# A two-layer hybrid block on one core: the sums over gate and up weights on VectorE, and weights split 1024 columns at a time

## The chip, the core and the metric

The kernel runs on one core of one Trainium2 chip. The core's engines have their own instruction queues, and each queue runs in order: PE (TensorE) multiplies matrices, DVE (VectorE), ACT (ScalarE) and POOL (GpSimd) work element by element, SP issues the DMAs. The metric is the device time of one execution in microseconds (us); lower is better.

## What is computed

Two layers over 512 tokens of 1024 features, in fp32. Each layer has two gated feed-forward networks, a token mixer of three kinds of heads between them, and a small gated embedding at its end. Only the feed-forward networks matter here; there are four, two a layer.

```python
D_MODEL, SEQ, DEPTH, D_FF = 1024, 512, 2, 2816

def swiglu(x, w_in, w_out):
    gate, up = jnp.split(x @ w_in, 2, axis=-1)
    return (jax.nn.silu(gate) * up) @ w_out

for l in range(DEPTH):
    x = x + 0.5 * rms_norm(swiglu(rms_norm(x, ln_ffn1_pre[l]), w_ffn1_in[l], w_ffn1_out[l]), ln_ffn1_post[l])
    mix = token_mixing(rms_norm(x, ln_mix_pre[l]), ...)
    x = x + rms_norm(mix, ln_mix_post[l])
    x = x + 0.5 * rms_norm(swiglu(rms_norm(x, ln_ffn2_pre[l]), w_ffn2_in[l], w_ffn2_out[l]), ln_ffn2_post[l])
    gate = jax.nn.sigmoid(rms_norm(x, ln_ple_pre[l]) @ w_ple_gate[l])
    x = x + rms_norm(gate * (p[l] @ w_ple_proj[l]), ln_ple_post[l])
```

## The kernel before

**Products in three parts.** Every fp32 operand of a large product is split into a high part (fp32r) and a low part, the rest: `split` (L140, L141) has ACT write the high part and DVE, or another engine if it is given, subtract it from the source. A product is then three matmuls (`mm3`, L162 to L164): high x high, high x low, low x high. A split of weights goes into a buffer of the pool `wsp`, tag `w`, which has NW buffers: six, for 512 columns each.

**The first product of a network** has 22 units (tiles), each of 128 gate and 128 up features. It goes by Winograd's form of Strassen's algorithm: instead of eight products of 128x512x256 there are seven, numbered 1 to 7, of 12 matmuls each (four blocks of inputs by three parts), so 84 in a unit. The price is sums. Those over inputs (`tx`) are made once for a network, in `turn`. Those over weights are made in each unit: from the raw weights g1, g2, u1, u2 (two tiles of a slot, 128x1024 each, by DMA) POOL makes s1 = u1 + u2 (L353), s2 = s1 - g1 (L354), s3 = g1 - u1 (L355) and s4 = g2 - s2 (L356), 512 columns each, into tiles `ws`. Products 1 and 2 take g1 and g2 as they are, 6, 7, 5, 3 and 4 take s2, s3, s1, s4 and u2. Each of the seven is split on its own, 512 columns.

**What comes out** is combined by DVE from PSUM: L362, L365, L367, L369, L370, L373, then ACT's silu (L371), then gate times up (L376). A PSUM bank serves two products: the first matmul of product 3 must wait until DVE has read product 6 out of the same bank (L362). ACT copies product 1 out (L347).

**What sets the order.** The program is written unit by unit; a scheduler then places the instructions on each queue, so DVE's queue mixes splits of the next unit with additions of this one. Nothing overtakes on a queue. Three of six raw slots (tag `q`) hold weights during the units; the other three hold `tx`. The first four units (G = 4) are loaded early, in `ffn_begin`, while the phase before ends, and their products 1 are given the splits that are made there, three or four of them by POOL; `NP1` and `flush` say between which of them the last tiles of tokens are turned and summed (`turn`).

**The second product** (`ffn_out`) goes pair by pair of feature tiles and by halves of the columns. Fourteen pairs of a network go by the seven products, with sums over features by POOL (`left`, L426 to L429), sums over weights by POOL and DVE (`right`, L448 to L450), and splits of the raw weights in two pieces of 256 and 512 columns (`wb`). The others are plain (`wblock`), split in two pieces of 512.

## Time and profile before

| | us |
|---|---|
| runs, median of 3 (lowest, highest) | 2371.92 (2371.49, 2373.13) |
| span of the profiled execution | 2369.3 |
| four networks, units 4 to 20 of each, a unit | about 11.2 |
| PE busy, DVE busy, POOL busy | 2142.1, 2019.5, 1215.5 |

The three runs were timed without the profile; the profiled execution is told by its span, from the first to the last instruction, which is 2.6 us below their median. The page's groups add up instructions of one line and shape: first the count, then busy time in us and the mean of one in ns, then the engine's idle time before them and what ended it.

```profile
L141 DVE TENSOR_TENSOR w<-wr,w 128x512 fp32r<-128x512 f32 x249 | 374.8, 1528 | 10.0 <-ACT w L140 9.8
L141 DVE TENSOR_TENSOR w<-ws,w 128x512 fp32r<-128x512 f32 x352 | 327.7, 935 | 3.2 <-ACT w L140 3.1
L354 POOL TENSOR_TENSOR ws<-ws,wr 128x512 f32<-128x512 f32 x88 | 147.4, 1675 | 0.6
```

Here `w` is a split's buffer, `wr` the raw weights, `ws` a sum, and `fp32r<-` the written and read types. Busy times overlap a little at their ends, so an operation's cost in a full queue is read from one start to the next.

### The profile page before, as it was taken

What the parts mean: (1) busy time and instruction counts of PE and PEld (TensorE: products, weight loads), DVE (VectorE), ACT (ScalarE), POOL (GpSimd) and SP (SyncE); (2) the same over time, 40 slices, a digit from 0 to 9 for tenths busy, and PEclk for the clock granted to TensorE, in tenths of its full rate; (3) what the DMA queues carried; (4) which work ended last, traced back from release to release, by engine and by line L of the source; (5) the groups of instructions that cost most, each with busy time, mean ns of one, the idle gap of its engine ahead of it and who ended that gap; (6) DMA issues with size and microseconds to landing.
All of it is one profiled execution on the core that took longest, in us unless ns stands there. A gap on an engine that the chain in (4) does not pass through costs nothing. (4 is left out here: it accounts for less than half of the span.)

```text
span 2369.3 us, 42540 instructions
## 1 busy us (share of the span) xinstructions
PE 2142.1 (90%) x16592; PEld 1975.2 (83%) x16592; DVE 2019.5 (85%) x2990; ACT 1159.0 (49%) x2262; POOL 1215.5 (51%) x1088
## 2 busy tenths in 40 slices
PE   5899988999998899988989989889999989989898
PEld 5888887988778888887878888888887789889787
DVE  8999999645768999998689999986557699999984
ACT  4444544546545444545554445444474454445443
POOL 5665476132236665566365655751332466555751
PEclk8999999999999999999999999999999999999999
DMA  3222222422031222123411221233220312222232
GB/s 151 90 89 90 71 90 90 147 81 55 20 142 54 86 93 90 63 90 116 134 71 72 92 105 55 84 120 122 68 63 7 143 72 90 90 90 75 78 107 80
DMA packets 67513, 208.78 MB, mean 88 GB/s; under 512 B 15728, under 2 KB 16752, under 8 KB 67312
## 3 DMA queue, kind: packets, MB, share of 16 engines
q1 hardware_dynamic: 67312, 206.07, 25.2%
q8 instruction: 130, 2.13, 0.4%
q14 instruction: 71, 0.58, 0.1%
HBM read 199.23 MB, written 6.82 MB: 87 GB/s over the span
## 5 line engine op out<-in xcount | busy, mean ns | idle before, releaser
L162 PE MATMUL p<-xh,w 128*128 128x256 f32 x1408 | 407.8, 291 | 79.8 <-DVE gate L362 77.5
L164 PE MATMUL p<-xh,w 128*128 128x256 f32 x1408 | 401.6, 286 | 13.6 <-DVE w L141 13.6
L163 PE MATMUL p<-xl,w 128*128 128x256 f32 x1408 | 400.8, 285 | 0.1
L141 DVE TENSOR_TENSOR w<-wr,w 128x512 fp32r<-128x512 f32 x249 | 374.8, 1528 | 10.0 <-ACT w L140 9.8
L140 ACT ACTIVATE w<-ws 128x512 fp32r<-128x512 f32 x352 | 210.6, 623 | 305.0 <-POOL ws L354 178.2
L162 PEld LDWEIGHTS p<-xh,w 128*128 128x128 f32 x1408 | 269.9, 192 | 95.5 <-DVE gate L362 89.7
L141 DVE TENSOR_TENSOR w<-ws,w 128x512 fp32r<-128x512 f32 x352 | 327.7, 935 | 3.2 <-ACT w L140 3.1
L162 PE MATMUL p<-tx,w 128*128 128x256 f32 x1056 | 299.9, 285 | 19.1 <-ACT tx L140 14.7
L164 PE MATMUL p<-tx,w 128*128 128x256 f32 x1056 | 298.9, 284 | 5.3 <-DVE w L141 5.2
L163 PE MATMUL p<-tx,w 128*128 128x256 f32 x1056 | 299.2, 284 | 4.7 <-DVE tx L141 4.7
L164 PEld LDWEIGHTS p<-xh,w 128*128 128x128 f32 x1408 | 270.9, 192 | 14.8 <-DVE w L141 14.8
L353 POOL TENSOR_TENSOR ws<-wr 128x512 f32<-128x512 f32 x88 | 119.0, 1352 | 316.2 <-issue 299.5
L163 PEld LDWEIGHTS p<-xl,w 128*128 128x128 f32 x1408 | 270.8, 192 | 0.7 <-DVE xl L141 0.7
L162 PEld LDWEIGHTS p<-tx,w 128*128 128x128 f32 x1056 | 204.7, 194 | 21.2 <-ACT tx L140 15.3
L164 PEld LDWEIGHTS p<-tx,w 128*128 128x128 f32 x1056 | 203.3, 193 | 7.4 <-DVE w L141 7.1
L163 PEld LDWEIGHTS p<-tx,w 128*128 128x128 f32 x1056 | 203.7, 193 | 5.6 <-DVE tx L141 5.6
L466 PE MATMUL y<-wo,hq 128*128 128x256 f32 x1536 | 189.4, 282 | 3.2 <-DVE up L373 2.7
L140 ACT ACTIVATE w<-wr 128x512 fp32r<-128x512 f32 x264 | 163.3, 625 | 57.7 <-PE p L164 41.9
L466 PEld LDWEIGHTS y<-wo,hq 128*128 128x128 f32 x1536 | 184.5, 189 | 4.8 <-DVE up L373 3.5
L355 POOL TENSOR_TENSOR ws<-wr 128x512 f32<-128x512 f32 x88 | 145.9, 1658 | 46.7 <-DVE w L141 45.0
L354 POOL TENSOR_TENSOR ws<-ws,wr 128x512 f32<-128x512 f32 x88 | 147.4, 1675 | 0.6
L356 POOL TENSOR_TENSOR ws<-wr,ws 128x512 f32<-128x512 f32 x88 | 142.4, 1618 | 5.6
(436 smaller groups left out, 5613.4 us busy)
## 6 DMA issues: line engine op xcount, KB each, us to landing
wr<-in_w_ffn_in SPq DMA_DIRECT2D x176, 512.0 KB, 4.1
ws_r<-in_w_ffn_out SPq DMA_DIRECT2D x56, 512.0 KB, 3.2
wo_r<-in_w_ffn_out SPq DMA_DIRECT2D x32, 512.0 KB, 3.3
pkrv_r<-in_w_rw SPq DMA_DIRECT2D x16, 512.0 KB, 3.5
wpg_r<-in_w_ple_gate SPq DMA_DIRECT2D x16, 512.0 KB, 3.4
xd<-x SPq DMA_DIRECT2D x8, 512.0 KB, 2.9
x<-xd SPq DMA_DIRECT2D x8, 512.0 KB, 3.5
pq_r<-in_w_q SPq DMA_DIRECT2D x8, 512.0 KB, 3.5
```

Of the source, the lines that this page charges most:

```text
L140: self.nc.scalar.activation(hi, src, AF.Copy)
L141: (eng or self.nc.vector).tensor_tensor(lo, src, hi.bitcast(F32), ALU.subtract)
L162: mm(out, a[0], b[0], start=first, stop=False)
L163: mm(out, a[0], b[1], start=False, stop=False)
L164: mm(out, a[1], b[0], start=False, stop=last)
L353: g_.tensor_tensor(s1, u1, u2, ALU.add)
L354: g_.tensor_tensor(s2, s1, g1, ALU.subtract)
L355: g_.tensor_tensor(s3, g1, u1, ALU.subtract)
L356: g_.tensor_tensor(s4, g2, s2, ALU.subtract)
L466: nc.tensor.matmul(banks[n][:, u], a[:, x, u * 128:u * 128 + 128], b[y], start=n not in seen, stop=last and i == 2, skip_group_check=True)
```

## The change

**Sums.** In `unit`, DVE makes the sums with other signs, so that all are additions: one operation of 1024 columns makes [g1 + u1, u1 + u2] (sx), two of 512 make [g1 + (u1 + u2), that + g2] (sy). POOL makes none. The signs are set right in `turn` (L241 in the new numbering), at the last subtraction and in the product of gate and up, which becomes a SCALAR_TENSOR_TENSOR.

**Splits.** g1 and g2 are split together (w12, products 1 and 2), sx (w75, products 7 and 5) and sy (w63, products 6 and 3) too, 1024 columns each; u2 alone goes to two tiles of another tag (w4, product 4). `wsp` has three buffers of 1024 columns, not six of 512. In `right` the raw weights are split in one piece of 768 columns, and `pack` lays them out for it; `wblock` splits its block whole. Products 1 and 2 of the first four units go together (`gate`), and `NFL` says before which of them the last tiles are turned.

```diff
-NQ, NH, NW = 6, 6, 6
+NQ, NH, NW = 6, 6, 3
...
-NP1 = 2
+NFL = {1: 1, 2: NT}
...
+    @staticmethod
+    def cut(q, c):
+        return [z[:, c] for z in q]
...
         if slot:
             w = self.slot("h", [2, c], name, F32R)
             self.split(w[:, 0], w[:, 1], raw, eng)
-            return [(w[:, 0, i * c // 2:(i + 1) * c // 2], w[:, 1, i * c // 2:(i + 1) * c // 2]) for i in range(2)]
-        return [self.wsplit(raw[:, i * c // 2:(i + 1) * c // 2], name, eng) for i in range(2)]
+            w = w[:, 0], w[:, 1]
+        else:
+            w = self.wsplit(raw, name, eng)
+        return [self.cut(w, slice(i * c // 2, (i + 1) * c // 2)) for i in range(2)]
...
-        v_.tensor_tensor(t1, ps[0], t1, ALU.subtract)
-        v_.tensor_tensor(t2, ps[1], t1, ALU.subtract)
+        v_.tensor_tensor(t1, t1, ps[0], ALU.subtract)
+        v_.scalar_tensor_tensor(t2, ps[1], -1.0, t1, ALU.mult, ALU.subtract)
         v_.tensor_tensor(t3, ps[1], t3, ALU.subtract)
-        g_.tensor_tensor(t4, t4, t2, ALU.subtract)
+        g_.tensor_tensor(t4, t4, t2, ALU.add)
...
-        self.ffn_w1 = [self.wsplit(r[:, 0, 0:512], "w1", None if self.first and not i else EW1) for i, r in enumerate(self.ffn_raw)]
+        self.ffn_w1 = [self.wsplit(r[:, 0], "w1", None if self.first and not i else EW1) for i, r in enumerate(self.ffn_raw)]
...
-            q = src if isinstance(src, tuple) else self.wsplit(src, f"w{n}", eng)
+        lo, hi = slice(0, 512), slice(512, 1024)
+        def product(n, q, out):
             for k in range(4):
                 self.mm3(out, [a[:, k * 128:(k + 1) * 128] for a in q], [b[:, k] for b in right[n]], k == 0, k == 3)
 
...
             r = self.ffn_raw[m] if m < G else self.ffn_load(l, w, [m])[0]
             return r, self.mm_tile("p12"), self.tmp.tile([128, S], F32, tag="tb0", name="gate", bufs=4)
 
-        def p1(r, pa, a):
-            product(1, r[:, 0, 0:512], pa[:, L])
-        def p2(m, r, pa, a, eng=None):
-            product(2, r[:, 0, 512:1024], pa[:, H], eng)
+        def gate(m, pa, a, q):
+            product(1, self.cut(q, lo), pa[:, L])
+            product(2, self.cut(q, hi), pa[:, H])
             a_.activation(a[:, (H, L)[m % 2]], pa[:, L], AF.Copy)
 
         def unit(m, r, pa, a):
-            g1, g2, u1, u2 = r[:, 0, 0:512], r[:, 0, 512:1024], r[:, 1, 0:512], r[:, 1, 512:1024]
-            ss = [self.wraw.tile([128, 1024], F32, tag="raw", name="ws") for _ in range(2)]
-            s1, s2, s3, s4 = (q[:, i * 512:(i + 1) * 512] for q in ss for i in range(2))
-            g_.tensor_tensor(s1, u1, u2, ALU.add)
-            g_.tensor_tensor(s2, s1, g1, ALU.subtract)
-            g_.tensor_tensor(s3, g1, u1, ALU.subtract)
-            g_.tensor_tensor(s4, g2, s2, ALU.subtract)
+            sx, sy = (self.wraw.tile([128, 1024], F32, tag="raw", name="ws") for _ in range(2))
+            v_.tensor_tensor(sx.rearrange("p (i c) -> p i c", i=2), r[:, :, lo],
+                             r[:, 1].rearrange("p (i c) -> p i c", i=2), ALU.add)
+            v_.tensor_tensor(sy[:, lo], sx[:, hi], r[:, 0, lo], ALU.add)
+            v_.tensor_tensor(sy[:, hi], sy[:, lo], r[:, 0, hi], ALU.add)
+            sx, sy = self.wsplit(sx, "w75"), self.wsplit(sy, "w63")
+            u2 = [self.tmp.tile([128, 512], F32R, tag="sg", name="w4") for _ in range(2)]
+            self.split(u2[0], u2[1], r[:, 1, hi])
             pc, pb, pd = self.aux_tile("p63"), self.aux_tile("p75"), self.mm_tile("p4")
             b = self.tmp.tile([128, S], F32, tag="tb1", name="up", bufs=2)
-            # an even tile has the tokens' second half first
             P, Q = (L, H) if m % 2 else (H, L)
-            product(6, s2, pc[:, L])
+            product(6, self.cut(sy, lo), pc[:, L])
             v_.tensor_tensor(a[:, Q], pc[:, L], a[:, P], ALU.add)
-            product(7, s3, pb[:, P])
-            product(5, s1, pb[:, Q])
+            product(7, self.cut(sx, lo), pb[:, P])
+            product(5, self.cut(sx, hi), pb[:, Q])
             v_.tensor_tensor(b.rearrange("p (i t) -> p i t", i=2), pb.rearrange("p (i t) -> p i t", i=2),
                              a[:, None, Q].to_broadcast([128, 2, 256]), ALU.add)
             v_.tensor_tensor(a[:, P], pa[:, H], a[:, P], ALU.add)
-            product(3, s4, pc[:, H])
+            product(3, self.cut(sy, hi), pc[:, H])
             v_.tensor_tensor(a[:, Q], pc[:, H], b[:, Q], ALU.add)
             v_.tensor_tensor(b[:, Q], pb[:, Q], b[:, P], ALU.add)
             a_.activation(a, a, AF.Silu)
             product(4, u2, pd[:, L])
-            v_.tensor_tensor(b[:, P], pd[:, L], b[:, P], ALU.add)
+            v_.tensor_tensor(b[:, P], b[:, P], pd[:, L], ALU.subtract)
             if m % 4 == 0:
                 hs.append(self.slot("h", [8, 256], "h"))
-            v_.tensor_tensor(hs[m // 4][:, m % 4 * 2:m % 4 * 2 + 2], a.rearrange("p (i t) -> p i t", i=2),
-                             b.rearrange("p (i t) -> p i t", i=2), ALU.mult)
-        EW2 = None
+            v_.scalar_tensor_tensor(hs[m // 4][:, m % 4 * 2:m % 4 * 2 + 2], b.rearrange("p (i t) -> p i t", i=2), -1.0,
+                                    a.rearrange("p (i t) -> p i t", i=2), ALU.mult, ALU.mult)
         first = [left(m) for m in range(G)]
-        for (r, pa, a), q in zip(first, self.ffn_w1):
-            if r is self.ffn_raw[NP1]:
-                self.flush(1)
-            product(1, q, pa[:, L])
+        for m, ((r, pa, a), q) in enumerate(zip(first, self.ffn_w1)):
+            if m in NFL:
+                self.flush(NFL[m])
+            gate(m, pa, a, q)
         self.flush()
-        for m, q in enumerate(first):
-            p2(m, *q, EW2)
         for m in range(NM):
-            q = first[m] if m < G else left(m)
+            r, pa, a = first[m] if m < G else left(m)
             if m >= G:
-                p1(*q)
-                p2(m, *q)
-            unit(m, *q)
+                gate(m, pa, a, self.wsplit(r[:, 0], "w12"))
+            unit(m, r, pa, a)
         wo = self.ins[f"w_ffn{w}_out"]
...
-                    for n, c in zip(((2, 3), (4, 8))[t // 2], (L, H)):
-                        add(n, t % 2, q[:, :, order[j][t // 2]], [z[:, c] for z in w[j]], last and j == 1)
+                    for n, c in zip(((2, 3), (4, 8))[t // 2], ((H, L), (L, H))[j]):
+                        add(n, t % 2, q[:, :, order[j][t // 2]], cut(w[j], c), last and j == 1)
...
-            e[4].tensor_tensor(sa, r[:, :, H], r[:, 0].rearrange("p (i d) -> p i d", i=2), ALU.subtract)
+            q = r.rearrange("p f (i d) -> p (f i) d", i=2)
+            e[4].tensor_tensor(sa, q[:, 0:4:3], q[:, 1::-1], ALU.subtract)
             e[5].tensor_tensor(sb[:, 0], r[:, 1, H], sa[:, 0], ALU.subtract)
             e[6].tensor_tensor(sb[:, 1], r[:, 1, L], sb[:, 0], ALU.subtract)
-            b0, b1 = self.wsplit(r[:, 0, L], "wb"), self.wsplit(r[:, 1], "wb")
+            bs = self.wsplit(r.rearrange("p f d -> p (f d)")[:, 256:1024], "wb")
             for i, q in enumerate((sa, sb)):
                 self.split(ts[:, 0, 2 * i:2 * i + 2], ts[:, 1, 2 * i:2 * i + 2], q)
-            cut = lambda q, c: [z[:, c] for z in q]
             tt = lambda i: [ts[:, e, i] for e in range(2)]
-            return {1: b0, 2: cut(b1, L), 3: cut(b1, H), 4: tt(3), 5: tt(0), 6: tt(2), 7: tt(1)}
+            return {1: cut(bs, L), 2: cut(bs, H), 3: cut(bs, slice(512, 768)), 4: tt(3), 5: tt(0), 6: tt(2), 7: tt(1)}
...
-        vg = [self.wsp.tile([128, 1056], F32, tag="w", name="vg") for _ in range(2)]
+        vg = self.wsp.tile([128, 2112], F32, tag="w", name="vg")
         off = 0
 
         def T(name, shape, **k):
             nonlocal off
             n = int(np.prod(shape[1:]))
-            i = off // 1056
-            if off + n > 1056 * (i + 1):
-                i, off = i + 1, 1056 * (i + 1)
-            t = vg[i][:, off - 1056 * i:off - 1056 * i + n]
+            t = vg[:, off:off + n]
...
-        wo = a[f"w_ffn{w}_out"].reshape(2, NM // 2, 2, 128, 2, 512)
-        o[f"w_ffn{w}_out"] = np.ascontiguousarray(wo.transpose(0, 4, 1, 3, 2, 5)).reshape(2, 2, NM // 2, 128, 1024)
+        wo = a[f"w_ffn{w}_out"].reshape(2, NM // 2, 2, 128, 2, 2, 256).transpose(0, 4, 1, 3, 2, 5, 6)
+        wo = np.stack([wo[:, :, :, :, 0, ::-1], wo[:, :, :, :, 1]], 4)
+        o[f"w_ffn{w}_out"] = np.ascontiguousarray(wo).reshape(2, 2, NM // 2, 128, 1024)
```

On DVE, the middle of a network, a unit's worth; `w1` to `w7` are splits named by their products, `p63`, `p75`, `p12` and `p4` PSUM banks. Before:

```order
L141 TENSOR_TENSOR w1_1980<-wr_1975,w1_1980 128x512
L362 TENSOR_TENSOR gate_1849<-p63_1887,gate_1849 128x256
L141 TENSOR_TENSOR w2_1995<-wr_1975,w2_1995 128x512
L367 TENSOR_TENSOR gate_1849<-p12_1848,gate_1849 128x256
L141 TENSOR_TENSOR w6_2021<-ws_2011,w6_2021 128x512
L365 TENSOR_TENSOR up_1890<-p75_1888,gate_1849 128x512
L141 TENSOR_TENSOR w7_2037<-ws_2012,w7_2037 128x512
L369 TENSOR_TENSOR gate_1849<-p63_1887,up_1890 128x256
L370 TENSOR_TENSOR up_1890<-p75_1888,up_1890 128x256
L141 TENSOR_TENSOR w5_2052<-ws_2011,w5_2052 128x512
L373 TENSOR_TENSOR up_1890<-p4_1889,up_1890 128x256
L141 TENSOR_TENSOR w3_2069<-ws_2012,w3_2069 128x512
```

The same place in the changed program (L368 is the former L362, L371 the former L365, L383 the former L376):

```order
L368 TENSOR_TENSOR gate_1982<-p63_2026,gate_1982 128x256
L383 SCALAR_TENSOR_TENSOR h_1856<-up_1909,gate_1862 128x512
L356 TENSOR_TENSOR ws_2251<-wr_2218 128x1024
L371 TENSOR_TENSOR up_2029<-p75_2027,gate_1982 128x512
L373 TENSOR_TENSOR gate_1982<-p12_1981,gate_1982 128x256
L141 TENSOR_TENSOR w63_2139<-ws_2132,w63_2139 128x1024
L141 TENSOR_TENSOR w4_2263<-wr_2218,w4_2262 128x512
L375 TENSOR_TENSOR gate_1982<-p63_2026,up_2029 128x256
L141 TENSOR_TENSOR w12_2223<-wr_2218,w12_2223 128x1024
L358 TENSOR_TENSOR ws_2252<-ws_2251,wr_2218 128x512
L376 TENSOR_TENSOR up_2029<-p75_2027,up_2029 128x256
L141 TENSOR_TENSOR w75_2256<-ws_2251,w75_2256 128x1024
```

The three sums (L356, L358, and L359 a row further) have come into DVE's queue between the splits, for the unit after next; fourteen operations make a unit in both.

On POOL, the network's entry in the first layer, from the sums of inputs (`tx`, `xr`) on. Before:

```order
L141 TENSOR_TENSOR tx<-xr,tx 128x4x128
L353 TENSOR_TENSOR ws<-wr 128x512
L355 TENSOR_TENSOR ws<-wr 128x512
L354 TENSOR_TENSOR ws<-ws,wr 128x512
L356 TENSOR_TENSOR ws<-wr,ws 128x512
```

After, where L430 and L432 are the second product's sums over features (L426 and L428 before):

```order
L243 TENSOR_TENSOR xr<-xr,tx 128x512
L141 TENSOR_TENSOR tx<-tx 128x4x128
L141 TENSOR_TENSOR tx<-xr,tx 128x4x128
L430 TENSOR_TENSOR hs<-h 128x256
L432 TENSOR_TENSOR hs<-h 128x256
```

Before, those four sums of weights follow each other 22 times in a network, and some stand in between the last `tx` operations; after, POOL's queue goes from `tx` straight to the second product.

On PE, all seven products of a unit stay. Between the last matmul of product 6 and the first of product 3, which waits for L362 (L368), its queue has 27 others before, and 26 to 45, mostly 34 to 42, after.

More of the change, by code (lines that the diff above doesn't have):

```diff
@@ L331, in ffn @@
         hs = []
-        def product(n, src, out, eng=None):
-            q = src if isinstance(src, tuple) else self.wsplit(src, f"w{n}", eng)
+        lo, hi = slice(0, 512), slice(512, 1024)
+        def product(n, q, out):
             for k in range(4):
@@ L403, in ffn_out @@
         L, H = slice(0, 256), slice(256, 512)
+        cut = self.cut
         raw = lambda b: hs[b // 2][:, 4 * (b % 2):4 * (b % 2) + 4]
```

## The prediction

> **What bounds the kernel now.** I read the page first: its engine totals, and DVE's slices, 40 of 59 us each.
>
> ```profile
> PE 2142.1 (90%) x16592; PEld 1975.2 (83%) x16592; DVE 2019.5 (85%) x2990; ACT 1159.0 (49%) x2262; POOL 1215.5 (51%) x1088
> DVE  8999999645768999998689999986557699999984
> ```
>
> DVE stands at 9 in four stretches, with 8 at their edges. These are the four feed-forward networks. Next I read the waits, for who holds PE up.
>
> ```profile
> PE p L162 <- DVE gate L362: 77.5, 66, 2.6
> ```
>
> PE loses 77.5 us to one DVE line, in 66 waits. So I read the timeline of one unit (one tile of 128 gate and 128 up features): first DVE, then POOL, then the ends of PE's part. Columns: start, busy time, engine, line, shape.
>
> ```profile
> 176.19 1.76 DVE L141 TENSOR_TENSOR w<-ws,w 128x512 fp32r<-128x512 f32 x1
> 177.87 0.68 DVE L376 TENSOR_TENSOR h<-gate,up 128x512 f32<-128x512 f32 x1
> 178.47 3.47 DVE L141 TENSOR_TENSOR w<-wr,w 128x512 fp32r<-128x512 f32 x2
> 181.87 0.41 DVE L362 TENSOR_TENSOR gate<-p,gate 128x256 f32<-128x256 f32 x1
> 182.20 1.43 DVE L141 TENSOR_TENSOR w<-wr,w 128x512 fp32r<-128x512 f32 x1
> 183.56 0.41 DVE L367 TENSOR_TENSOR gate<-p,gate 128x256 f32<-128x256 f32 x1
> 183.89 0.68 DVE L141 TENSOR_TENSOR w<-ws,w 128x512 fp32r<-128x512 f32 x1
> 184.49 0.68 DVE L365 TENSOR_TENSOR up<-p,gate 128x512 f32<-128x512 f32 x1
> 185.09 0.68 DVE L141 TENSOR_TENSOR w<-ws,w 128x512 fp32r<-128x512 f32 x1
> 185.69 0.41 DVE L369 TENSOR_TENSOR gate<-p,up 128x256 f32<-128x256 f32 x1
> 186.14 0.42 DVE L370 TENSOR_TENSOR up<-p,up 128x256 f32<-128x256 f32 x1
> 186.48 0.68 DVE L141 TENSOR_TENSOR w<-ws,w 128x512 fp32r<-128x512 f32 x1
> 187.08 0.42 DVE L373 TENSOR_TENSOR up<-p,up 128x256 f32<-128x256 f32 x1
> 187.41 1.76 DVE L141 TENSOR_TENSOR w<-ws,w 128x512 fp32r<-128x512 f32 x1
> ```
>
> ```profile
> 176.07 1.33 POOL L353 TENSOR_TENSOR ws<-wr 128x512 f32<-128x512 f32 x1 [4.21 <-issue]
> 178.03 1.68 POOL L355 TENSOR_TENSOR ws<-wr 128x512 f32<-128x512 f32 x1 [0.63 <-DVE w L141]
> 179.67 1.73 POOL L354 TENSOR_TENSOR ws<-ws,wr 128x512 f32<-128x512 f32 x1
> 181.47 1.61 POOL L356 TENSOR_TENSOR ws<-wr,ws 128x512 f32<-128x512 f32 x1
> ```
>
> ```profile
> 182.34 0.39 PE L162 MATMUL p<-xh,w 128*128 128x256 f32 x1 [1.02 <-DVE gate L362]
> 182.56 0.28 PE L163 MATMUL p<-xl,w 128*128 128x256 f32 x1
> 192.23 0.28 PE L164 MATMUL p<-tx,w 128*128 128x256 f32 x1
> ```
>
> A unit takes 187.41-176.19 = **11.22 us**, and DVE has no gap in it. One and the same split (128x512, L141) goes from start to start in 0.60 us while POOL is silent (183.89 to 184.49). Beside a POOL sum it takes 1.68, 1.70 twice and 1.36 us. These four cost 6.44 instead of 2.40, so 4.04 us of the unit is stretching. The additions that read PSUM (L362) keep their 0.41 us even beside the sum at 181.47. PE's 83 rows from 182.56 to 192.23 lie 9.67/82 = 0.118 us apart; 84 of them are **9.91 us**, and the rest of the unit is PE's wait for L362, which stands behind two stretched splits. DVE bounds the unit, and POOL's sums make DVE long.
>
> **The change, part by part: the units.** POOL's four sums go, and with them the 4.04 us. DVE gets the sums as one operation of 1024 columns and two of 512. Of seven splits of 512 columns, six become three of 1024. For that size, and for SCALAR_TENSOR_TENSOR, which replaces the product at the unit's end, the nearest rows are these, with POOL silent beside the first:
>
> ```profile
> 271.18 1.72 POOL L356 TENSOR_TENSOR ws<-wr,ws 128x512 f32<-128x512 f32 x1
> 273.70 1.21 DVE L141 TENSOR_TENSOR hq<-h,hq 128x1024 fp32r<-128x1024 f32 x1
> 274.84 0.41 DVE L367 TENSOR_TENSOR gate<-p,gate 128x256 f32<-128x256 f32 x1
> 8.51 1.41 DVE L202 SCALAR_TENSOR_TENSOR xn<-x,r,ln_ffn_pre 128x512 f32<-128x512 f32 x2 [2.88 <-DMA ln_ffn_pre<-in_ln_ffn_pre]
> 258.81 1.06 ACT L140 ACTIVATE hq<-h 128x1024 fp32r<-128x1024 f32 x1 [2.63 <-DVE w L141]
> ```
>
> 1024 columns: 1.14 us from start to start; a SCALAR_TENSOR_TENSOR: 0.67 (two in 1.41, less the overlap of 0.08 that 0.68 against 0.60 shows, by two). DVE's unit after is 3 x 1.14 + 0.60 for the splits, 1.14 + 2 x 0.60 for the sums, 0.60 + 0.33 + 0.33 + 0.45 + 0.34 + 0.33 for the six that read PSUM, and 0.67: **9.41 us**, below PE's 9.91. So PE becomes the bound, by half a microsecond.
>
> The Trainium skill's page SBUF — State Buffer, section "SBUF: two separate sides", says that a DVE operation with two SBUF inputs and a GpSimd one exclude each other for the whole instruction. The rows agree. In the second product, below, this rule speaks against a gain.
>
> *The added waits.* Three wide buffers replace six narrow ones. In the built program the split for products 6 and 3 takes the buffer of its own unit's products 1 and 2, so ACT must wait until PE has read that. Between that reader and product 6 stand 24 or 33 other matmuls in turn in PE's new order, at least 24 x 0.118 = 2.8 us, against 1.06 on ACT and 1.21 on DVE. Products 7 and 5 have a buffer to themselves, with 34 or more between (4.0 us). Behind the waiting split on DVE stand the small split, L375 and the next sums; the sums run a unit ahead and can give way. So 0.5 us is left for DVE's queue, and more in every other unit. I cost the waits at nothing; where DVE's queue is longer, PE pays what is beyond.
>
> I take **10.1 us** a unit: 9.91, 0.1 for a restart as at 182.34 (0.22 us to the next matmul, not 0.118), and 0.1 for a short wait. Bounds: 9.91 and 10.9 (the 1.02 us wait stays). How many units:
>
> ```profile
> 88.11 1.77 DVE L376 TENSOR_TENSOR h<-gate,up 128x512 f32<-128x512 f32 x1
> 279.96 0.69 DVE L376 TENSOR_TENSOR h<-gate,up 128x512 f32<-128x512 f32 x1
> 764.20 0.69 DVE L376 TENSOR_TENSOR h<-gate,up 128x512 f32<-128x512 f32 x1
> 791.17 1.78 DVE L376 TENSOR_TENSOR h<-gate,up 128x512 f32<-128x512 f32 x1
> ```
>
> Unit 3 ends at 88.11, unit 20 at 279.96: 17 units in 191.85 us, 11.29 each. Four networks: 68 x (11.29-10.1) = **-81 us** (bounds -94 and -27).
>
> **The first four units of a network.** Their products 1 and 2 come earlier, so a unit has 60 matmuls (7.07 us), and DVE, without one wide split, 9.41-1.14 = 8.27 us: DVE stays the bound. Now it is (791.17-764.20)/3 = 8.99. Three intervals save 2 us, four networks -8. At the entry PE waits for the sums of the inputs, tx:
>
> ```profile
> 749.73 0.58 PE L162 MATMUL p<-tx,w 128*128 128x256 f32 x1 [4.16 <-ACT tx L140]
> 752.04 0.58 PE L163 MATMUL p<-tx,w 128*128 128x256 f32 x1 [1.73 <-DVE tx L141]
> ```
>
> POOL's sums no longer stand between its tx operations, but its four first weight splits grow to 1024 columns and DVE gets 1.14 + 1.20 of sums there. Between -5.9 (both waits gone) and +5 (the sums, 2.3, and two POOL splits, each longer by a POOL operation's 1.33) I take -1 a network, near zero since both move at once. Together **-12 us** (-32 to +20).
>
> **The second product.** In each of 56 pairs the splits of 256 and 512 columns become one of 768.
>
> ```profile
> L141 DVE TENSOR_TENSOR wb<-ws_r,wb 128x512 fp32r<-128x512 f32 x56 | 74.8, 1335 | 2.8 <-ACT wb L140 2.8
> L141 DVE TENSOR_TENSOR wb<-ws_r,wb 128x256 fp32r<-128x256 f32 x56 | 42.5, 759 | 0.0
> L141 DVE TENSOR_TENSOR xh<-h,xh 128x768 fp32r<-128x768 f32 x28 | 36.3, 1295 | 0.0
> 283.00:420.00 137.00, 117.39 (x908) 111.54 (x907) 131.60 (x152) 69.33 (x124) 90.65 (x77) 0.98 0.29 94
> ```
>
> By the means a pair saves 1.335 + 0.759 - 1.295 = 0.80 us, 45 in all. But undisturbed it is only one start, 2 x 0.60 - 1.14 = 0.06 us, 3 in all. The window's columns are length, then busy time of PE, PEld, DVE, ACT, POOL: DVE is busy 131.60 of 137 us and POOL 90.65, so much of those means is DVE standing behind POOL's operations, which all remain. I take **-8 us**, near the low end (-3 to -45). By the Trainium skill's lock, POOL's time would be paid however DVE's work is cut, and the term would be the 3.
>
> PE stands nearly without gaps in the mixers, so wider splits there count as nothing; a chain that starts on a fresh split can lose 1.14 - 0.60 = 0.5 us a few times. Sum: 81 + 12 + 8 = **101 us**. The trace's span is 2369.3 us, the median of the runs 2.6 above it; 2371.9 - 101 = **2271 us**.
>
> **The rivals.**
> *The wait stays.* PE meets a DVE that works through two wide splits before the PSUM addition, and loses 1.02 us as now. For it: DVE has only 0.5 us to spare in 9.91. Against: between product 6 and the matmul that needs this addition stand 27 others before (3.2 us), and after mostly 34 to 42 (at least 4.0 us). 68 x (11.29-10.93) = 24, with 12 and 8 half paid: 2371.9 - 34 = 2338 us. Chance 0.14.
> *The second product pays in full*, 45 rather than 8, since DVE is the bound there: 2234 us. Against: POOL's work stays. Chance 0.08.
> *Slower: a full engine gets more work.* If the splits at L141 are long for what they read and not for POOL, DVE's unit is 9.41 + 4.04 = 13.45 us: 68 x (13.45-11.29) = +147, 2519 us. It decides from 1.88 us of stretching that stays. Against: the same split takes 0.68 at 183.89. Chance 0.04. The Trainium skill's page Perfetto Trace Analysis, section "Optimizing Scalar/DVE Operations", speaks for this one: a saturated DVE may be relieved by giving work to GpSimd. It adds that their shared port may undo the help.
> *No gain.* The change moves what it says (POOL's queue has no sum left), but raw weights could come late: three slots, two loads a unit.
>
> ```profile
> wr<-in_w_ffn_in SPq DMA_DIRECT2D x176, 512.0 KB, 4.1
> ```
>
> Two in turn take 8.2 us of a 10 us unit. If freeing a slot and loading it came to the old 11.2 us, nothing would change: 2372 us. Against: a slot is free as soon as its small split is done, over a unit ahead of the sums that read the next load. Chance 0.04.
>
> **How the numbers follow.** The forecast has the remaining 0.70, with a range of its own of 2245 to 2300 (a unit of 9.91 and entries that gain, to one of 10.5). The range runs from 2235, just above the full second product, to 2340, just above the stayed wait; it leaves out the other three rivals, 0.16, and a little of the forecast's own edges. Faster by over 0.2% (4.7 us, about what a measurement of this kernel can tell from no change): 0.92; within: 0.04; slower: 0.04.
>
> **What would show it.** From one L383 to the next, 10.1 us in the middle of each network. L141 of 128x1024 at 1.2 us mean there, L356 the same, L358 and L359 at 0.68. POOL without work between the network's entry and its second product. PE's 77.5 us on L362 (now L368) below 15. I am wrong if splits beside a silent POOL still take over 1.3 us, if PE waits for ACT's hi parts of the wide buffers, or if the networks' ends give back what the units save.

## The result, and the profile after

The changed kernel takes **2287.2 us** (median of 4 runs, 2286.8 to 2288.4) against 2371.7 (4 runs, 2369.8 to 2373.1): 0.9646 of the time, interval 0.9632 to 0.9659. It is faster by 84 us where 101 were forecast. The profiled execution has a span of 2285.0 us.

The page of the changed kernel, engine totals and the slices of DVE and POOL, 40 of 57 us each:

```profile
PE 2135.1 (93%) x16592; PEld 1978.8 (87%) x16592; DVE 1872.9 (82%) x2870; ACT 1108.4 (49%) x1869; POOL 718.4 (31%) x728
DVE  8999998555768999998689999985557699999984
POOL 4000476132234000576230006750422330007741
```

DVE is still at 9 in the networks, so that row alone would not tell that the bound has moved. POOL has gaps of three zeros in each network: these are the units. The windows do tell. Columns: length, then busy time (instructions) of PE, PEld, DVE, ACT, POOL, granted clock, DMA share, GB/s. First the kernel before, then the changed one, in the middle of the first network:

```profile
180.00:220.00 40.00, 35.79 (x298) 34.97 (x297) 39.86 (x52) 17.01 (x31) 21.91 (x14) 1.00 0.30 106
```

```profile
180.00:220.00 40.00, 40.00 (x339) 40.00 (x338) 36.78 (x56) 18.14 (x25) 0.00 (x0) 1.00 0.26 90
```

DVE's 39.86 of 40 us became 36.78, PE's 35.79 became 40.00 with 339 matmuls instead of 298: PE bounds the units. Groups of the changed kernel (busy, mean ns, idle before and what ended it):

```profile
L168 PE MATMUL p<-xh,w 128*128 128x256 f32 x1408 | 400.3, 286 | 4.4 <-DVE gate L368 2.4 <-ACT xh L140 1.6 <-ACT w L140 0.4
L168 PE MATMUL p<-tx,w 128*128 128x256 f32 x1056 | 296.3, 284 | 9.4 <-ACT tx L140 7.8 <-ACT w L140 1.7
L141 DVE TENSOR_TENSOR w<-ws,w 128x1024 fp32r<-128x1024 f32 x176 | 220.9, 1255 | 17.6 <-ACT w L140 16.5
L356 DVE TENSOR_TENSOR ws<-wr 128x1024 f32<-128x1024 f32 x88 | 112.4, 1278 | 6.1 <-DMA wr<-in_w_ffn_in 5.8
L141 DVE TENSOR_TENSOR wb<-ws_r,wb 128x768 fp32r<-128x768 f32 x56 | 84.5, 1509 | 2.5 <-ACT wb L140 2.5
```

PE's wait for the gate addition, 77.5 us before, is 2.4 us, and 1024 columns take 1.26 us. The ends of units 3 and 20 in the timeline, first and second network:

```profile
85.34 0.68 DVE L383 SCALAR_TENSOR_TENSOR h<-up,gate 128x512 f32<-128x512 f32 x1
255.39 0.73 DVE L383 SCALAR_TENSOR_TENSOR h<-up,gate 128x512 f32<-128x512 f32 x1
766.81 0.69 DVE L383 SCALAR_TENSOR_TENSOR h<-up,gate 128x512 f32<-128x512 f32 x1
938.20 0.71 DVE L383 SCALAR_TENSOR_TENSOR h<-up,gate 128x512 f32<-128x512 f32 x1
```

Seventeen units take 170.05 and 171.39 us, 10.0 and 10.1 each. The same marks cut the whole span into stages, and this table (us, summed over four networks, two mixers and two embedding stages) is how all runs are read below. An entry goes from the last update of x (L249, after L255) of the stage before to the end of unit 0.

| stage | before | after | difference |
|---|---|---|---|
| entries | 149.1 | 163.8 | +14.7 |
| unit 0 to 3 | 109.0 | 98.1 | -10.9 |
| unit 3 to 20 | 767.6 | 684.2 | -83.4 |
| unit 20 to the network's end | 644.8 | 630.9 | -13.9 |
| mixers | 584.5 | 594.8 | +10.3 |
| embedding stages | 110.5 | 109.5 | -1.0 |

The sum is -84.2, as much as the spans differ.

The marks are DVE's, and DVE's order against PE's has changed. At the end of unit 20 PE has 66 or 67 matmuls of the first product still to start before, and 13 or 14 after. So the table is read together with a second cut, at the end of PE's last matmul of the first product: up to there the four networks take 1057.9 us before and 964.0 after (-93.9), and from there on 612.6 and 613.1. The first product brought the whole gain, the second product nothing, and the mixers gave 10.3 us back.

### The profile page after: what moved, and what is told of

Read it like the earlier page. It is cut to its first block, busy times and chain, and to the rows that moved or that the text cites. A ratio compares the mean times of both kernels' runs of the same rounds, so it can differ in the third digit from the quotient of the medians.

```text
span 2285.0 us, 41245 instructions
## 1 busy us (share of the span) xinstructions
PE 2135.1 (93%) x16592; PEld 1978.8 (87%) x16592; DVE 1872.9 (82%) x2870; ACT 1108.4 (49%) x1869; POOL 718.4 (31%) x728
## 4 chain that ended last, share of the span: by engine, by line
PE 61%; DVE 19%; POOL 8%; issue 5%; ACT 5%; DMA 1%; SPq 0%; DVEq 0%; POOLq 0%; ACTq 0%
PE p L170 12%; PE p L169 12%; PE p L168 12%; DVE xl L141 3%; DVE wt L141 3%; PE y L471 2%; DVE wb L141 2%; DVE xh L141 2%; DVE wt_r L455 1%; PE pkrv L170 1%; PE pkrv L169 1%; PE pkrv L168 1%; DVE xn L208 1%; POOL hs L431 1%; POOL hs L430 1%
## 5 line engine op out<-in xcount | busy, mean ns | idle before, releaser
L168 PE MATMUL p<-xh,w 128*128 128x256 f32 x1408 | 400.3, 286 | 4.4 <-DVE gate L368 2.4
L430 POOL TENSOR_TENSOR hs<-h 128x256 f32<-128x256 f32 x48 | 61.6, 1284 | 834.1 <-PE p L169 813.9
L168 PE MATMUL p<-tx,w 128*128 128x256 f32 x1056 | 296.3, 284 | 9.4 <-ACT tx L140 7.8
L169 PE MATMUL p<-tx,w 128*128 128x256 f32 x1056 | 295.0, 283 | 6.7 <-DVE tx L141 6.7
L170 PE MATMUL p<-tx,w 128*128 128x256 f32 x1056 | 294.3, 283 | 2.5 <-DVE w L141 2.5
L168 PEld LDWEIGHTS p<-xh,w 128*128 128x128 f32 x1408 | 271.3, 193 | 6.5 <-DVE gate L368 3.2
L140 ACT ACTIVATE w<-ws 128x1024 fp32r<-128x1024 f32 x176 | 186.0, 1057 | 155.8 <-PE p L170 147.1
L141 DVE TENSOR_TENSOR w<-ws,w 128x1024 fp32r<-128x1024 f32 x176 | 220.9, 1255 | 17.6 <-ACT w L140 16.5
L168 PEld LDWEIGHTS p<-tx,w 128*128 128x128 f32 x1056 | 201.9, 192 | 11.9 <-ACT tx L140 9.0
L140 ACT ACTIVATE w<-wr 128x512 fp32r<-128x512 f32 (+1 forms) x176 | 147.8, 844 | 116.8 <-PE p L170 62.0
L471 PE MATMUL y<-wt,xh 128*128 128x256 f32 x768 | 126.4, 301 | 35.2 <-DVE wt L141 16.3
L141 DVE TENSOR_TENSOR w<-wr,w 128x512 fp32r<-128x512 f32 (+1 forms) x161 | 150.6, 939 | 3.3 <-ACT w L140 2.7
L471 PEld LDWEIGHTS y<-wt,xh 128*128 128x128 f32 x768 | 109.1, 204 | 43.5 <-DVE wt L141 18.3
L141 DVE TENSOR_TENSOR wt<-wt_r,wt 128x512 fp32r<-128x512 f32 x112 | 122.8, 1121 | 0.0
```

Source lines behind the costliest of these rows:

```text
L140: self.nc.scalar.activation(hi, src, AF.Copy)
L141: (eng or self.nc.vector).tensor_tensor(lo, src, hi.bitcast(F32), ALU.subtract)
L168: mm(out, a[0], b[0], start=first, stop=False)
L169: mm(out, a[0], b[1], start=False, stop=False)
L170: mm(out, a[1], b[0], start=False, stop=last)
L430: e[0].tensor_tensor(s1, r[:, 0], r[:, 3], ALU.add)
```

## The experiments

Theory: POOL's sums made DVE's operations long, and their removal is the gain. Rivals: the wider splits are the gain; or DVE was long for another reason.

| kernel | median us (range) | ratio to before, interval | entries | 0 to 3 | 3 to 20 | 20 to end | mixers |
|---|---|---|---|---|---|---|---|
| e1 sums on DVE, narrow | 2260.9 (2257.9-2264.4) | 0.9537, 0.9523-0.9551 | 159.5 | 103.5 | 667.6 | 628.4 | 582.2 |
| e2 sums on POOL, wide | 2322.4 (2317.5-2323.2) | 0.9792, 0.9777-0.9806 | 172.8 | 110.6 | 701.5 | 627.6 | 594.8 |
| e3 changed, idle POOL work | 2506.1 (2505.7-2506.5) | 1.0571, 1.0550-1.0592 | 180.2 | 125.8 | 855.8 | 633.7 | 595.3 |
| e4 changed, second sums on DVE | 2226.1 (2223.8-2233.2) | 0.9399, 0.9381-0.9417 | 162.1 | 98.5 | 692.8 | 571.2 | 591.9 |
| e5 changed, halved splits | 2281.8 (2278.2-2283.1) | 0.9624, 0.9610-0.9638 | 166.7 | 115.0 | 692.3 | 600.4 | 589.2 |
| e6 all sums on DVE, narrow | 2210.3 (2207.7-2213.8) | 0.9326, 0.9312-0.9340 | 157.8 | 102.3 | 658.6 | 598.2 | 583.4 |
| e7 e6, entries on DVE | 2205.0 (2203.8-2205.6) | 0.9301, 0.9285-0.9316 | 152.0 | 102.3 | 662.1 | 595.4 | 582.8 |
| e8 e6, units 0-3 on POOL | 2218.1 (2216.2-2218.8) | 0.9356, 0.9342-0.9370 | 148.2 | 117.3 | 665.1 | 593.1 | 582.8 |
| e9 changed, 256 + 512 | 2287.5 (2285.7-2287.8) | 0.9647, 0.9632-0.9661 | 162.9 | 98.0 | 684.2 | 630.0 | 596.5 |
| e10 e2, halved splits | 2397.3 (2395.0-2402.0) | 1.0117, 1.0100-1.0134 | 167.3 | 120.6 | 754.4 | 643.4 | 594.5 |
| e11 e7, mixers' wo on DVE | 2238.6 (2236.2-2240.2) | 0.9441, 0.9427-0.9455 | 156.3 | 99.3 | 662.2 | 591.9 | 615.2 |

The scheduler makes each program's order anew, so a mark can shift against PE's work (against the changed kernel, e5 has 30 us less behind unit 20 and 28 more ahead of it).

**Sums on DVE alone (e1).** From the kernel before:

```
-            g_.tensor_tensor(s1, u1, u2, ALU.add)
+            v_.tensor_tensor(s1, u1, u2, ALU.add)
...
```

> The kernel before with one edit: the four sums of gate and up weights run on DVE instead of POOL; splits stay 512 columns wide with six buffers. Theory (the sums' place is the gain): seven splits and four sums of 0.60 us, 2.38 that read PSUM and 0.60 at the end make 9.58 us of DVE a unit, below PE's 9.91, so units take about 10.1 us as in the changed kernel, while mixers keep the order of before: 2262 us (2250 to 2290), faster than the changed kernel. Rival (the width of the splits is needed): units stay above 10.6 us, 2325 us or more.

Measured 2260.9 us. Units 3 to 20 take 9.82 us each, and the mixers 582.2 us, 584.5 before: with narrow splits the gain is 110 us, more than the whole change brings. The width is not needed. By the second cut the first product takes 935.6 us here, 122.3 less than before, and the rest of the networks 623.5, which is 10.9 more with the same second product; why is not shown.

**Work on POOL that nobody waits for (e3).** Into the changed kernel, units 4 to 21:

```
+                for i in range(4):
+                    g_.tensor_tensor(jk[:, i % 2], r[:, 0, lo], r[:, 1, lo], ALU.add)
```

> The changed kernel plus work that nothing uses: in units 4 to 21 POOL adds 512 columns of raw gate to 512 of raw up weights, four times a unit, into a tile that is free there. Nothing waits for these sums. Theory (DVE's operations between SBUF tiles stand behind POOL's): DVE's unit grows from 9.41 by about 4, splits and sums at L141, L356, L358 get longer, the three or four additions that read PSUM stay at 0.42 us; a unit takes 13 to 14.5 us, the total rises by 200 to 300 us to about 2520. Rival (before, DVE was long for the order in which its operands came, not for POOL's presence): no change, 2287 us.

Measured 2506.1 us. The groups of this run, to set beside the 1255 and 1278 ns above, with two that had 1217 and 419 in the changed kernel:

```profile
L397 POOL TENSOR_TENSOR jk<-wr 128x512 f32<-128x512 f32 x288 | 536.0, 1893 | 407.3 <-DMA wr<-in_w_ffn_in 407.2
L141 DVE TENSOR_TENSOR w<-ws,w 128x1024 fp32r<-128x1024 f32 x176 | 267.1, 1517 | 5.4 <-ACT w L140 5.4
L356 DVE TENSOR_TENSOR ws<-wr 128x1024 f32<-128x1024 f32 x88 | 122.9, 1397 | 5.7 <-DMA wr<-in_w_ffn_in 5.4
L141 DVE TENSOR_TENSOR w<-wr,w 128x1024 fp32r<-128x1024 f32 x73 | 129.4, 1772 | 2.6 <-ACT w L140 2.6
L375 DVE TENSOR_TENSOR gate<-p,up 128x256 f32<-128x256 f32 x88 | 36.4, 413 | 1.8 <-PE p L170 1.8
```

DVE's busy time rises from 1872.9 to 2119.5 us with not one instruction more on it: 246.6/288 = 0.86 us for each POOL operation. The additions that read PSUM keep their 0.41. So POOL's presence makes the stretching, not the order in which operands come. The total came out as expected, the unit below it: 12.59 us where 13 to 14.5 were expected.

**Sums on POOL, splits wide (e2) or halved (e10).** In e2 the changed kernel's three sums go to POOL. In e10 its splits are halved besides:

```
-            v_.tensor_tensor(sx.rearrange(...
+            g_.tensor_tensor(sx.rearrange(...
...
+        for i in range(n):
+            s = slice(i * c // n, (i + 1) * c // n)
+            self.split(w[:, 0, s], w[:, 1, s], src[:, s], eng)
```

> The changed kernel with one edit: its three sums a unit run on POOL; splits stay 1024 wide, three buffers. Theory (place): DVE has 7.07 us of its own a unit and stands behind POOL's sums for 3.5 to 4.5 more, so a unit is 10.6 to 11.6 us, splits at L141 of 1024 columns have a mean of 1.8 us or more (1.26 in the changed kernel), total 2360 us (2325 to 2395). Rival (width): units stay at 10.1 us and the time at 2290.

> The changed kernel with two edits: its three sums a unit on POOL, and splits of 1024 columns made as two of 512. With wide splits and sums on POOL the time was 2322 us and units 10.3 us; the kernel before has four sums on POOL, seven narrow splits and 11.3 us. Theory (each POOL operation holds DVE up once, for 0.8 to 1.0 us whatever the split's width; there are three instead of four): DVE 7.3 of its own and 2.4 to 3.0, units 10.3 us, total about 2318 us (2305 to 2335). Rival (the width was it: more and shorter DVE operations are caught more often): units 11 us or more, 2350 us or more.

Measured 2322.4 and 2397.3 us: the theory's price was wrong both times, and in e10 the rival's range came true. The unit is 10.32 us in e2, below what was expected, and 11.09 in e10, where the rival said 11. The groups of e2, then of e10:

```profile
L141 DVE TENSOR_TENSOR w<-ws,w 128x1024 fp32r<-128x1024 f32 x176 | 311.6, 1771 | 7.3 <-ACT w L140 5.8
L141 DVE TENSOR_TENSOR w<-wr,w 128x1024 fp32r<-128x1024 f32 x73 | 116.3, 1593 | 1.0 <-ACT w L140 1.0
L141 DVE TENSOR_TENSOR w<-wr,w 128x512 fp32r<-128x512 f32 x88 | 108.5, 1233 | 0.0
L383 DVE SCALAR_TENSOR_TENSOR h<-up,gate 128x512 f32<-128x512 f32 x88 | 104.8, 1191 | 1.0
```

```profile
L141 DVE TENSOR_TENSOR w<-ws,w 128x512 fp32r<-128x512 f32 x352 | 376.6, 1091 | 7.1 <-ACT w L140 7.1
L141 DVE TENSOR_TENSOR w<-wr,w 128x512 fp32r<-128x512 f32 x234 | 256.6, 1120 | 0.3 <-ACT w L140 0.3
L387 DVE SCALAR_TENSOR_TENSOR h<-up,gate 128x512 f32<-128x512 f32 x88 | 127.2, 1445 | 0.8
```

Against 0.68 and 1.21 us undisturbed, e2 is stretched by 2 x 0.56 + 0.38 + 0.55 + 0.51 = 2.6 us a unit, e10 by 4 x 0.41 + 3 x 0.44 + 0.77 = 3.7. The same three sums on POOL cost DVE 1.1 us more where its splits are short. So a POOL operation has no fixed price, and wide splits do shelter DVE while POOL works. They take units 3 to 20 from 754.4 (e10) to 701.5 us, and by the second cut the first product from 1066.7 to 999.7. Once POOL is silent they bring nothing there: by that cut, whose mark does not move against PE's work, e5 with halved splits takes 960.9 us and the changed kernel 964.0.

**The second product's sums on DVE (e4, e6).** One line, in the changed kernel and in e1:

```
-SE = "0000010"
+SE = "1111111"
```

> The changed kernel with one edit: the sums of the second product (seven a pair, six of them on POOL) all run on DVE. Theory (the same one): by the means of the changed kernel DVE's operations in the second product are about 175 us longer than undisturbed ones of their size, and the sums cost DVE some 115 us at 0.33 us for 256 columns and 0.60 for 512; DVE, the bound there, saves up to 60 us: 2245 us (2225 to 2275). Rival (a full engine gets more work): slower, 2330 us or more.

> The kernel before with the sums of both products on DVE and nothing else: narrow splits, six buffers. If both gains come from taking POOL's sums away from DVE, they add up: 2261 us with the first product's sums alone, less the 43 us of the second products and some 13 at the last unit of a network, where the second product's first sums already run: 2205 us (2190 to 2225), faster than the changed kernel by some 80. Rival (with its narrow splits DVE is too full in the second product): 2235 us or more.

Measured 2226.1 and 2210.3 us. In e4 the networks take 52.6 us less than in the changed kernel, 51.7 of them behind PE's last matmul of the first product, the embedding stages 6.8 less. In all it is 61 us faster, about the most that was worked out, where 42 were expected. Its groups (1509, 1121 and 1178 ns in the changed kernel):

```profile
L141 DVE TENSOR_TENSOR wb<-ws_r,wb 128x768 fp32r<-128x768 f32 x56 | 57.6, 1028 | 0.3 <-ACT wb L140 0.3
L141 DVE TENSOR_TENSOR wt<-wt_r,wt 128x512 fp32r<-128x512 f32 x112 | 78.3, 705 | 0.0
L141 DVE TENSOR_TENSOR xl<-hs,xl 128x512 fp32r<-128x512 f32 x40 | 27.1, 687 | 0.0
```

A nearly full engine was given 304 operations more and its busy time fell, from 1872.9 to 1846.6 us. The gains add up in e6, which beats the changed kernel by 77 us.

**The 768-column split by itself (e9).** In the changed kernel:

```
-            bs = self.wsplit(... [:, 256:1024], "wb")
+            for c in (slice(0, 256), slice(256, 768)):
+                self.split(bs[:, 0, c], bs[:, 1, c], rf[:, 256 + c.start:256 + c.stop])
```

> The changed kernel with one edit: the split of 768 columns in the second product is made as 256 and 512, as before, in the same buffer. It prices the one split by itself. From the end of unit 20 to the end of a network the changed kernel takes 630.9 us over four networks. By the prediction's term this grows by 8 us (2295 us in all), by the start saved alone by 3 (2290), by the busy times of the rows of before by 45 (2332). The busy time of one pair's wb splits is 1.51 us in the changed kernel.

Measured 2287.5 us, no change. The groups of e9:

```profile
L141 DVE TENSOR_TENSOR wb<-ws_r,wb 128x512 fp32r<-128x512 f32 x56 | 61.1, 1091 | 0.0
L141 DVE TENSOR_TENSOR wb<-ws_r,wb 128x256 fp32r<-128x256 f32 x56 | 55.6, 993 | 5.9 <-ACT wb L140 5.9
```

DVE's wb splits are busy for 116.7 instead of 84.5 us and the end of the network does not move (630.0 against 630.9). Undisturbed, a second start in 56 pairs would be 3 us. DVE's busy time as a whole rises by 17.6 us only, from 1872.9 to 1890.5, so part of the 32 us has left other groups. The account that these are times spent behind POOL, which move from one operation to another, fits this; it is not shown operation by operation.

**Halved splits (e5).** The changed kernel with the loop shown for e10, sums on DVE.

> The changed kernel with one edit: every split of 1024 columns into a buffer of the ring of three is made as two of 512 columns, in the same buffer. It tells apart why the two mixers take 594.8 us there and 585.2 in the kernel before (from the last update of x of one network to that of the mixer). Width (a chain of matmuls that starts on a fresh split waits for all 1024 columns): mixers come back to 582 to 588, total about 2276 us. Ring (three buffers instead of six, each held until its last half is read): mixers stay at 592 to 598, total 2283 to 2292. The units have DVE at 9.6 us instead of 9.4, still below PE, and should not move.

Measured 2281.8 us, mixers 589.2: between the two. (The 585.2 of the expectation starts one update of x too early; between the last updates it is 584.5.) In e10, whose mixers have the same halved splits, they take 594.5, and in e9, whose mixers are untouched, 596.5. Six narrow buffers gave 582.2 to 584.5 in all five kernels that have them without other edits there; three wide ones gave 591.9 to 596.5 in five. So the pair (wide, three buffers) costs the mixers about 10 us. Width's share is 0.3 (e10 against e2) to 5.6 of it (e5 against the changed kernel), and the rest, the ring or the order that it leads to, stays open: a ring of another size was not run.

**The entries (e7, e8).** From e6, e7 moves POOL's entry work to DVE, e8 leaves the first units' sums on POOL:

```
-        EB, E1, E3, E4 = None, g_, g_, g_
+        EB, E1, E3, E4 = None, v_, v_, v_
...
-        EW1 = self.nc.gpsimd
+        EW1 = self.nc.vector
```

```
+            e_ = g_ if m < G else v_
-            v_.tensor_tensor(s1, u1, u2, ALU.add)
+            e_.tensor_tensor(s1, u1, u2, ALU.add)
...
```

> The kernel with all sums on DVE, and at the entries of the networks no work on POOL either: the first four weight splits and the four operations on the inputs' sums (tx, xr, xl) of each of the last two token tiles go to DVE. Theory carried to the entries (POOL's operation of about 1.3 to 1.7 us holds DVE up for longer than the 0.60 us that DVE needs for it): the four entries, 159.5 us with the first product's sums on DVE, fall to 150 or less, total 10 us below the kernel with all sums on DVE. Rival (the entry waits on one chain of operations, in which POOL does its part while DVE has other work): entries 165 or more, total 5 us or more above it.

> The kernel with all sums on DVE, except that units 0 to 3 of each network leave their four sums on POOL, as before. The four entries took 149.1 us before and 159.5 with the first product's sums on DVE; units 0 to 3 took 109.0 and 103.5. If DVE's sums of the first units stand in front of the inputs' sums there, the entries come back to 148 to 152 and units 0 to 3 to 109, together 5 us less. If the order of PE's products at the entry, which the scheduler has changed, costs the 10 us, the entries stay near 160.

e7: 2205.0 us, entries 152.0. The sign is the theory's, at half its size, and all of it lies in the first entry (57.1 to 51.2 us). The intervals of the two ratios overlap by a hair. e8: entries 148.2, as before the change, units 0 to 3 15.0 us longer than in e6, and the whole 8 us slower. By the expectation the first of these would be the sign that DVE's sums stand in front there, but a count of matmuls does not bear it out. When unit 0 ends, PE has started 669 matmuls of the first product in the four entries of e8 and 796 in those of e6; these 127 are 15 us at 0.118, more than the 9.6 by which the entries are shorter, and PE waits longer in them (44.5 against 37.0 us). By the end of unit 3, e8 is 5.4 us later and has 62 matmuls fewer done. So the mark moved, not the work, and e8 does not decide between its two explanations. The trace of the changed kernel shows the crowding at its third entry: two operations of POOL, then DVE, then PE.

```profile
1156.03 2.85 POOL L141 TENSOR_TENSOR w<-wr,w 128x1024 fp32r<-128x1024 f32 x1
1158.83 1.74 POOL L141 TENSOR_TENSOR xl<-xr,xh 128x512 fp32r<-128x512 f32 x1
```

```profile
1156.54 4.58 DVE L208 SCALAR_TENSOR_TENSOR xn<-x,r,ln_ffn_pre 128x512 f32<-128x512 f32 x2
...
1167.80 0.67 DVE L240 TENSOR_TENSOR xr<-xr,xtp 128x512 f32<-128x512 f32 x1
1168.40 0.68 DVE L358 TENSOR_TENSOR ws<-ws,wr 128x512 f32<-128x512 f32 x1
1169.00 1.21 DVE L141 TENSOR_TENSOR w<-ws,w 128x1024 fp32r<-128x1024 f32 x1
1170.13 0.68 DVE L241 SCALAR_TENSOR_TENSOR tx<-xtp,xr 128x512 f32<-128x512 f32 x1
```

```profile
1171.53 0.58 PE L168 MATMUL p<-tx,w 128*128 128x256 f32 x1 [4.59 <-ACT tx L140]
1175.94 0.58 PE L169 MATMUL p<-tx,w 128*128 128x256 f32 x1 [2.75 <-DVE tx L141]
```

Two normalisations that take 1.41 us undisturbed take 4.58 beside POOL's two operations. Later a sum and a wide split, 1.7 us, stand between two steps of the chain that PE waits for. And PE is slow between its waits: with a granted clock of 0.50 its matmuls follow each other in 0.213 us, not 0.118 as at 1.00.

```profile
1162.00:1166.60 4.60, 4.60 (x23) 4.60 (x22) 4.60 (x4) 0.00 (x0) 2.46 (x2) 0.50 0.33 114
```

**Where the rule ends (e11).** From e7, `OW = "1111"` becomes `"0000"`.

> The kernel with all sums and the entries on DVE, and besides the splits of the mixers' output weights (wo, and wot of the first half) on DVE instead of POOL. It asks where the rule ends: in the mixers DVE is busy some 60 per cent and PE has nearly no gap, so POOL's work there costs nothing that shows. Mixers stay at 582.8 us within 3, the total at 2205 within 4. If POOL's operations cost as much there as in the networks (0.9 us each, 16 of them, less 0.6 on DVE), it is 5 us faster.

Measured 2238.6 us: both expectations missed, the mixers take 615.2 us, 16 more each. In the trace of e11 PE waits near the first mixer's end, where its longest wait in e7 is 0.9 us:

```profile
657.67 1.09 PE L966 MATMUL pyt<-ident,x 128*128 128x128 f32 x4 [4.95 <-DVE x L959]
668.29 1.33 PE L162 MATMUL y<-wot,xh 128*128 128x512 f32 x3 [2.06 <-ACT wot L140]
```

The scheduler also put the mixers' pieces in another order in this program. Whether the splits on DVE or that order cost the 32 us is not told apart by this run.

## Why the prediction was right, and where it was off

**What bounds, and the stretching.** Right. DVE bounded the unit, and e3 shows that POOL's operations stretch DVE's. What e2 and e10 add: the 4.04 us were not the price of POOL's sums alone, but of POOL's sums beside seven short splits. Either edit alone takes most of the excess over PE's floor: units take 9.82 us with the sums moved and narrow splits (e1), and 10.32 with wide splits and POOL's sums (e2). That e2 has three sums and not four seems to matter little, since with halved splits the three leave the unit at 11.09 (e10; 11.29 before). The prediction credited the place and gave the width 0.06 us for each joined pair. Together they could not show it, since PE's floor caps both.

**The units.** 10.1 us and -81 predicted, 10.06 and -83.4 measured. That PE becomes the bound is right. The two tenths that were added to its floor, for a restart and for a short wait, fit by luck: between the ends of units 3 and 20 PE has no gap in any network. Here is the second one (columns as above):

```profile
767.00:938.00 171.00, 171.00 (x1440) 171.00 (x1439) 160.98 (x239) 81.26 (x107) 3.84 (x3) 1.00 0.28 99
```

One matmul follows another in 118.9 ns there, not 118, so 84 take 9.99 us, and the marks enclose 1441 matmuls in networks 2 to 4, which is 17.15 units. What went is visible on PE: before, from the end of unit 3 to its last matmul of the first product, it waited 78.8 us over the four networks, and another 16 went to 164 matmuls of the first product that followed in about 0.217 us instead of 0.118. After, there is nothing of either.

**The added waits of the ring** cost nothing in the units, as predicted: PE's waits on ACT's hi parts (ACT w) are 0.4 and 1.7 us in the two groups of L168. The sentence that wider splits in the mixers "count as nothing" failed: the mixers pay 10.3 us. Whether that is width or ring is open.

**The first four units.** -12 predicted. Units 0 to 3 gave 10.9 (8 predicted), but the entries lost 14.7 where -1 a network was chosen. The waits are not what failed: over the four entries PE waits 41.0 us, 45.3 before, a fall of 4.3 where 4 were predicted. Its waits for tx fell from 19.4 to 14.5, and POOL's wider first splits made it wait 7.5 that it had not waited before. But PE is busy for 123.0 us there instead of 103.9. Of these 19 us some 8.4 are only moved, since 71 more matmuls of the first product come ahead of the mark. Another 7.4 are time lost: 152 matmuls of the first product instead of 74 follow in 0.213 us, the step of the window with granted clock 0.50 above. No term of the prediction had that; why there are more of them is open.

**The second product.** -8 predicted. From PE's last matmul of the first product to the end of the networks the kernels take 612.6 us before and 613.1 after, and e9, with the split back in two pieces, 611.3: the split is worth nothing that was measured. The step that failed took part of the busy means as cost. The Trainium skill's page SBUF — State Buffer, section "SBUF: two separate sides", whose exclusion of DVE and GpSimd would have left 3 us, is nearer to the runs.

**Left out of the sum.** The last unit was in no term. Its interval, from unit 20 to 21, shortened by 14.6 us over the four networks (20 us before, 16 after, in each), but most of that is the shift of the marks: 53 matmuls a network have moved ahead of unit 20, 25 us in all at 0.118. With the last unit in, the first product gave 93.9 us where 81 + 12 were predicted. That the sum fits so well is luck in part, as the terms show. The 17 us by which the whole fell short are, but for 1 or 2, the 8 of the second product and the 10.3 of the mixers.

**The rivals.** PE's wait for the gate addition is gone (2.4 us); late raw weights held the sums at L356 up for 5.8 us in all; and the kernels whose full DVE got more work became faster (e1, e4 and e6). On that last one, the Trainium skill's page Perfetto Trace Analysis, section "Optimizing Scalar/DVE Operations", says that giving work of a saturated DVE to GpSimd may make sense, and that the port they share may undo it. The runs bear out the second half: a sum of 512 columns costs DVE 0.60 us if DVE does it, and 0.86 (e3) to 1.01 (4.04/4, before) if POOL does. Beside wide splits the two prices nearly meet: 2.6 us a unit for three sums on POOL (e2) against 1.14 + 2 x 0.60 = 2.34 on DVE.

The best kernel of the study is not the change but e7: the kernel before with every sum and the entries' work on DVE, 0.9301 of the time (0.9285 to 0.9316); e6, at 0.9326, is hardly apart from it.

## What to carry to other kernels

Before giving work of a full DVE to POOL, read one and the same DVE operation with POOL silent and with POOL busy. If the difference per POOL operation exceeds what DVE would need for that work itself, take the work back. This was seen where DVE was full; e11 took work back where it was not, and became slower for a reason that is open. A long busy time of an operation beside POOL is no price for that operation: in e9 32 us of it came back and the kernel took the same time. Where another engine's floor lies just below, two remedies for one wait do not add, so try each alone; here the simpler one was worth more than both. And where a mark is set by one engine, count the other's work between two marks before calling a stage longer or shorter.

## What was not expected of the hardware

POOL's operations stretch as well. With wide splits on DVE (e2) POOL's three sums take 2596, 1626 and 1860 ns, with short ones (e10) 2489, 1547 and 1589:

```profile
L356 POOL TENSOR_TENSOR ws<-wr 128x1024 f32<-128x1024 f32 x88 | 228.5, 2596 | 202.9 <-DVE w L141 200.6 <-DVE wpg L141 2.3
L359 POOL TENSOR_TENSOR ws<-ws,wr 128x512 f32<-128x512 f32 x88 | 163.7, 1860 | 6.6
L358 POOL TENSOR_TENSOR ws<-ws,wr 128x512 f32<-128x512 f32 x88 | 143.1, 1626 | 133.6 <-DVE w L141 131.1 <-DVE wpg L141 2.3
```

```profile
L360 POOL TENSOR_TENSOR ws<-wr 128x1024 f32<-128x1024 f32 x88 | 219.0, 2489 | 288.8 <-DVE w L141 286.5 <-DVE wpg L141 2.3
L363 POOL TENSOR_TENSOR ws<-ws,wr 128x512 f32<-128x512 f32 x88 | 139.8, 1589 | 6.6
L362 POOL TENSOR_TENSOR ws<-ws,wr 128x512 f32<-128x512 f32 x88 | 136.2, 1547 | 137.5 <-DVE w L141 134.0 <-DVE wpg L141 2.0 <-DVE rope L1268 1.5
```

Beside the longer DVE operations POOL's three are 0.46 us longer a unit, although e2 is the faster kernel of the two.

With PE gapless at a granted clock of 1.00, the changed kernel passes 339 matmuls in the window shown at the top, and e1 343 in the same window:

```profile
180.00:220.00 40.00, 40.00 (x343) 40.00 (x343) 38.81 (x74) 19.21 (x36) 0.00 (x0) 1.00 0.30 109
```

Between the ends of units 3 and 20 a matmul follows another in 118.9 ns on average in the changed kernel and, waits left out, in 117.7 in e1, so 84 of them take 9.99 and 9.89 us. Most of the difference lies in the matmuls over tx, the sums of the inputs: 118.1 ns from one to the next in the changed kernel, 115.9 in e1. All six kernels that have six narrow buffers show 115.7 to 116.3 ns there, and all seven that have three wide ones 118.0 to 118.2, e5 and e10 with their halved splits among them. So it is neither the width of the splits nor the place of the sums. It goes with the buffers, or with something else in which the two families of kernels differ; which of these is open.
